# A hybrid encoder layer on one core: low halves of four row sums formed in gate and up, and the finishing of the last down chunk in a paced list

## The chip, the cores and the metric

The kernel runs on one core of a Trainium2 chip. The time is device microseconds of one execution, as the median of three runs. Five engines work beside each other, each in the order of its own queue: TensorE (PE; PEld is its weight load), VectorE (DVE), ScalarE (ACT), GpSimd (POOL) and SyncE (SP), which only issues transfers. ScalarE and GpSimd issue some transfers too.

## What is computed

```python
def hybrid_layer(x, conv_prev, S0, sc_prev, ...):
    h = rmsnorm(x, norm_mix_pre)
    P = h @ w_in
    ...
    mix = jnp.concatenate([o, sc_out.astype(x.dtype)], axis=-1) @ w_o
    x = x + rmsnorm(mix, norm_mix_post)

    h = rmsnorm(x, norm_ffn_pre)
    f = (jax.nn.silu(h @ w_gate) * (h @ w_up)) @ w_down
    x = x + rmsnorm(f, norm_ffn_post)
    return x, conv_new, S_new, sc_new
```

There are 2048 + 128 rows of 1024 columns, in 17 tiles of 128 rows; D_FF is 2816, in 22 blocks of 128. The change touches only the last line of the layer and the product by `w_down` before it.

## The kernel before

A float32 product is made of three products of a shorter type, fp32r: each operand is split into a high half (a cast by ScalarE) and a low half (the operand less its high half, a subtraction by GpSimd or VectorE), and high by high, high by low and low by high are added up in PSUM. Over that, products of 2 by 2 blocks are done with seven multiplications instead of eight (Winograd's form of Strassen's method), with sums of blocks as operands.

**Gate and up.** `gate_up` (L1417) runs over three groups of row tiles (`FGROUPS`: 6, 6 and 5 tiles, called group 0, 1 and 2) and in each over the 22 blocks f. A step has seven products of 12 matmuls (L1396), 384 columns wide in groups 0 and 1 and 320 in group 2. ScalarE copies three of the four PSUM banks out (L1428 to L1430) before TensorE adds to them again. The weights (`fw`) lie in a ring of 12 pairs of halves (`NWB`), seven for a step; in groups 1 and 2 four of seven are loaded ready from `fsplit` (L1369) and three are split on the spot (L1371, L1372). Every second step VectorE forms in the tile `pt` (one buffer) six of the seven row sums that the down projection needs as operands; they are stored to `partd` (L1433, on ScalarE's queue) in the next step. Between groups `ffn_prep` (L1319, L1320) splits the next group's inputs.

**Down.** The loop at L1699 takes the 22 blocks in five chunks; the last has six of them, so that a product has 3 x 3 = 9 matmuls, each 512 columns wide (L1574). In a chunk it goes over eight pairs of row blocks (three each of groups 0 and 1, two of group 2; the first two, the duo, alternate) and over a single block, which in the last chunk comes before the last pair. `down_pair` (L1616) loads the seven row sums (`ar`, L1564, three buffers), `split` (L1551) makes the halves `as` (ring of six, `NDA`): the cast on ScalarE (L1554), the low half in the last chunk on VectorE for product 0 and on GpSimd for products 1 to 6 (L1557). VectorE adds each product to the accumulators (L1534).

**Finishing.** In the last chunk a pair ends with `finish` (L1577) for each of its two row blocks. For each half of 512 columns: ScalarE's sum of squares (L1587), an addition of EPS in the first half (L1589), the product by the norm's gain (L1590). Then the two sums are added (L1593), GpSimd takes the power -1/2 (L1594), VectorE scales each half and adds the residual row `xr` (L1599), and the half is stored to `out_y` (L1601). `xr` is loaded from `x2d` (L1548, tag `dr`, four buffers). The final pair has its own order of steps: products 0, 1, 2, 3, 5, 4, 6, and parts of `finish` between them (L1644, L1650, L1651).

The order in the queues isn't written out in full: a scheduler with a model of the engines places the instructions, within the dependences and the `issue_after` marks.

```python
steps = ((b1, True, a4), (b2, True, a4), (b3, True, a4), (b4, True, a4), (b1, False, a1), (b2, False, a2), (b3, False, a3))
...
e = V if i in ((0,) if end else (0, 3)) or (duo and not ch and len(ready) < 2) else G
```

## Time and profile before

| | us |
|---|---|
| median of 3 runs (2452.22 to 2453.81) | 2452.97 |
| the profiled execution, its own time | 2450.11 |
| its span | 2448.2 |
| TensorE busy | 2424.2 (99%) |
| VectorE busy | 1620.6 (66%) |
| ScalarE busy | 1043.0 (43%) |
| GpSimd busy | 572.7 (23%) |

The span runs from the first to the last recorded instruction of the profiled execution; what the execution's own time has over it, 1.9 us, lies around it. TensorE's granted clock is 0.999 of full speed over the whole span. In a row of instructions, `fbank<-dw,as` means that `fbank` is written from `dw` and `as`; after `x` comes how many there are. The last down chunk takes the stretch from about 2307 us on, the last group of gate and up ends near 1960.

### The profile page before, as it was taken

What the parts mean: (1) busy time and instruction counts of PE and PEld (TensorE: products, weight loads), DVE (VectorE), ACT (ScalarE), POOL (GpSimd) and SP (SyncE); (2) the same over time, 40 slices, a digit from 0 to 9 for tenths busy, and PEclk for the clock granted to TensorE, in tenths of its full rate; (3) what the DMA queues carried; (4) which work ended last, traced back from release to release, by engine and by line L of the source; (5) the groups of instructions that cost most, each with busy time, mean ns of one, the idle gap of its engine ahead of it and who ended that gap; (6) DMA issues with size and microseconds to landing.
All of it is one profiled execution on the core that took longest, in us unless ns stands there. A gap on an engine that the chain in (4) does not pass through costs nothing.

```text
span 2448.2 us, 39317 instructions
## 1 busy us (share of the span) xinstructions
PE 2424.2 (99%) x14360; PEld 2219.0 (91%) x14360; DVE 1620.6 (66%) x3070; ACT 1043.0 (43%) x2335; POOL 572.7 (23%) x664
## 2 busy tenths in 40 slices
PE   9999999999999999999999999999999999999997
PEld 7888889999989988899999999999999988887876
DVE  7875755746667356888888744456555565677698
ACT  6645546546444333444343422224333355333343
POOL 1101001001110000156655200000000056456664
PEclk9999999999999999999999999999999999999999
DMA  7774655766776657698877888888998744333475
GB/s 271 260 252 167 218 194 198 247 220 231 271 252 247 214 177 230 200 341 297 291 257 256 293 258 263 257 251 271 312 294 278 248 142 122 117 107 120 140 232 175
DMA packets 263465, 561.38 MB, mean 229 GB/s; under 512 B 25188, under 2 KB 144680, under 8 KB 245992
## 3 DMA queue, kind: packets, MB, share of 16 engines
q1 hardware_dynamic: 147024, 487.24, 59.1%
q10 hardware_dynamic: 116024, 70.58, 9.6%
q8 instruction: 113, 1.85, 0.3%
q0 software_dynamic: 224, 1.05, 0.1%
q14 instruction: 80, 0.66, 0.1%
HBM read 400.09 MB, written 158.70 MB: 228 GB/s over the span
## 4 chain that ended last, share of the span: by engine, by line
PE 87%; DVE 6%; issue 2%; DMA 2%; POOL 2%; ACT 1%; DVEq 0%; ACTq 0%; POOLq 0%; SPq 0%
PE fbank L1396 35%; PE dbank L317 26%; PE fbank L1574 11%; PE dbank L1161 4%; PE tbank L1161 4%; DVE xr L1599 1%; DVE acc L1534 1%; PE tbank L375 1%; POOL as L1557 1%; PE gbank L598 1%; PE gbank L605 1%; POOL dw L1246 1%; PE obank L777 1%; PE gbank L769 1%; PE ftbank L1190 1%
## 5 line engine op out<-in xcount | busy, mean ns | idle before, releaser
L1396 PE MATMUL fbank<-xh,fw 128*128 128x384 f32 (+1 forms) x3696 | 897.5, 326 | 0.7 <-ACT m L1428 0.6
L317 PE MATMUL dbank<-hi,w 128*128 128x384 f32 (+1 forms) x2240 | 655.5, 363 | 1.5 <-ACT w L296 0.8
L1396 PEld LDWEIGHTS fbank<-xh,fw 128*128 128x128 f32 x3696 | 650.8, 188 | 1.4 <-ACT m L1428 0.9
L1396 PE MATMUL fbank<-xl,fw 128*128 128x384 f32 (+1 forms) x1848 | 601.9, 326 | 0.0
L317 PEld LDWEIGHTS dbank<-hi,w 128*128 128x128 f32 x2240 | 412.5, 188 | 42.6 <-issue 3.6
L1574 PE MATMUL fbank<-dw,as 128*128 128x512 f32 x1782 | 420.8, 392 | 5.4 <-DVE acc L1534 2.9
L1574 PEld LDWEIGHTS fbank<-dw,as 128*128 128x128 f32 x1782 | 333.0, 188 | 85.1 <-POOL as L1557 3.5
L317 PE MATMUL dbank<-lo,w 128*128 128x384 f32 (+1 forms) x1120 | 399.6, 357 | 0.3 <-DVE lo L232 0.3
L1396 PEld LDWEIGHTS fbank<-xl,fw 128*128 128x128 f32 x1848 | 346.9, 188 | 0.0
L317 PEld LDWEIGHTS dbank<-lo,w 128*128 128x128 f32 x1120 | 210.7, 188 | 16.7 <-DVE lo L232 0.6
L1557 POOL TENSOR_TENSOR as<-ar,as 128x256 fp32r<-128x256 f32 (+1 forms) x202 | 183.5, 919 | 177.7 <-ACT as L1554 162.0
L1534 DVE TENSOR_TENSOR acc<-acc,fbank 128x512 f32<-128x512 f32 x246 | 164.0, 681 | 90.6 <-PE fbank L1574 77.2
L1246 POOL TENSOR_TENSOR dw<-dr,dw 128x512 fp32r<-128x512 f32 x48 | 70.1, 1472 | 504.2 <-ACT dw L1244 503.9
L1554 ACT CAST as<-ar 128x256 fp32r<-128x256 f32 (+1 forms) x287 | 116.5, 427 | 165.7 <-PE fbank L1574 123.0
L1371 ACT CAST fw<-rg 128x512 fp32r<-128x512 f32 x124 | 77.2, 622 | 233.8 <-PE fbank L1396 136.3
L321 DVE SCALAR_TENSOR_TENSOR acc<-R,vec,acc 128x512 f32<-128x512 f32 (+2 forms) x180 | 121.0, 673 | 28.6 <-ACT acc L358 22.7
L1444 DVE TENSOR_TENSOR c<-u,fbank 128x384 f32<-128x384 f32 (+1 forms) x66 | 34.9, 528 | 97.8 <-PE fbank L1396 97.8
L1440 DVE TENSOR_TENSOR m<-m,m 128x384 f32<-128x384 f32 (+1 forms) x44 | 23.1, 526 | 84.3 <-ACT m L1430 84.1
L1447 ACT ACTIVATE c<-c 128x384 f32<-128x384 f32 (+1 forms) x66 | 33.4, 506 | 97.5 <-DVE c L1446 97.5
L1372 POOL TENSOR_TENSOR fw<-rg,fw 128x512 fp32r<-128x512 f32 x44 | 64.1, 1458 | 45.4 <-ACT fw L1371 45.1
L350 POOL COPY hist<-R 128x3 f32<-128x3 f32 x60 | 20.0, 334 | 218.6 <-ACT R L326 169.3
L1442 ACT ACTIVATE m<-fbank 128x384 f32<-128x384 f32 (+1 forms) x66 | 31.2, 473 | 91.3 <-PE fbank L1396 74.4
(398 smaller groups left out, 3567.1 us busy)
## 6 DMA issues: line engine op xcount, KB each, us to landing
w<-wsplit SPq DMA_DIRECT2D x105, 1024.0 KB, 5.1
fw<-fsplit SPq DMA_DIRECT2D x188, 512.0 KB, 4.9
fsplit<-fw SPq DMA_DIRECT2D x94, 512.0 KB, 3.6
partd<-pt ACTq DMA_DIRECT2D x86, 384.0 KB, 5.8
rg<-in_w_gu SPq DMA_DIRECT2D x62, 512.0 KB, 4.3
wsplit<-w SPq DMA_DIRECT2D x28, 1024.0 KB, 5.2
wr<-in_w_in SPq DMA_DIRECT2D x34, 512.0 KB, 6.2
ar<-partd SPq DMA_DIRECT2D x43, 384.0 KB, 3.2
```

The lines of the kernel that those rows point to most:

```text
L317: T.matmul(ps[:, :c], l[:, k, :], r[k][:, :c], start=(k == 0 and r is hi and l is wh), stop=(k == KD - 1 and l is wl))
L321: r = V.scalar_tensor_tensor(acc, raw(d), w[:, d:d + 1], acc, op0=ALU.mult, op1=ALU.add)
L1161: T.matmul(pss[n], m_[:, j, :], w_[k][:, n * 512:(n + 1) * 512], start=(k == 0 and ci == 0), stop=(k == KD - 1 and ci == 2))
L1246: e.tensor_tensor(out=w[1], in0=v, in1=w[0].bitcast(F32), op=ALU.subtract)
L1371: A.copy(w[:, 0], v)
L1372: e.tensor_tensor(out=w[:, 1], in0=v, in1=w[:, 0].bitcast(F32), op=ALU.subtract)
L1396: T.matmul(ps, w_[:, c], b_[k][:, :hw], start=(first and k == 0 and ci == 0), stop=(k == KH - 1 and ci == 2), skip_group_check=not first)
L1444: V.tensor_add(c21, u2, b3)
L1534: return eng.tensor_tensor(out=dst, in0=dst, in1=ps, op=ALU.add)
L1554: ins = A.copy(a[:, 0, :n], v)
L1557: e.tensor_tensor(out=a[:, 1, :n], in0=v, in1=a[:, 0, :n].bitcast(F32), op=ALU.subtract)
L1574: T.matmul(ps, a[:, x_, q * P:(q + 1) * P], w[y_], start=(start and q == 0 and ci == 0), stop=(q == c - 1 and ci == 2), skip_group_check=True)
```

## The change

- In gate and up, for the last chunk of groups 1 and 2, the low halves of row sums 1 to 4 (`NLOW`) are formed one step after the sums: ScalarE casts each into a spare buffer of `a11` or `a21`, GpSimd subtracts it in place in `pt`, and a step later the result is stored to a new array `lowd` on ScalarE's queue. That is three bundles in group 1 and two in group 2, of whose third part nothing is formed ahead (`low_end`). In the down chunk `split` loads these low halves by SP into `as`; group 1 needs no subtraction for products 1 to 4 any more, group 2 one of 128 columns.
- The finishing steps become single functions. Those on VectorE go into a list, `todo`; after each addition to an accumulator `pace` issues up to two of them, and stops behind a factor. The sums of squares stay with the step that ends their half. EPS is added in the instruction that adds the two sums.
- In the last pair `issue_after` marks fix the order of products 5, 4 and 6 on TensorE and of the steps on VectorE; the gained halves go into the accumulators of the first pair instead of the tile `xm`, and only the first half of the last row block is stored by ScalarE's queue.

```diff
 NDA = 6
+NLOW = 4
...
+    lowd = {gi: dram.tile([len(g) // 2, P, NLOW, len(FCHUNKS[-1]) // 2, P], F32, name=f"lowd{gi}")
+            for gi, g in enumerate(FGROUPS) if gi}
...
+        def low_end(gi):
+            return len(FCHUNKS[-1]) // 2 - (gi + 1 == len(FGROUPS))
...
+                while lstores:
+                    nc.scalar.dma_start(**lstores.pop(0))
...
+            if lows:
+                pgi, pq, pp = lows.pop()
+                pw = len(FGROUPS[pgi]) * P // 2
+                his = [fb.tile([P, HW], F32R, tag=nm, name="hi_" + nm, bufs=2) for nm in ("a11", "a21")]
+                with tc.issue_after(gmark["A"].ins), tc.issue_after(gmark["V"].ins):
+                    for i in range(NLOW):
+                        A.copy(his[i % 2][:, :pw], pp[:, i, :pw])
+                        G.tensor_tensor(out=pp[:, i, :pw], in0=pp[:, i, :pw], in1=his[i % 2][:, :pw].bitcast(F32), op=ALU.subtract)
+                for j in range(len(FGROUPS[pgi]) // 2):
+                    lstores.append(dict(out=lowd[pgi][j, :, :, pq, :], in_=pp[:, 0:NLOW, j * P:(j + 1) * P]))
...
+                if gi and ch + 1 == len(FCHUNKS) and q < low_end(gi):
+                    lows.append((gi, q, pt))
...
-        def split(v, e, first=False):
+        def split(v, e, first=False, low=None):
             n = v.shape[-1]
             a = da.tile([P, 2, MC * P // 2], F32R, tag="as", name="as", bufs=NDA)
+            m = 0
+            if low is not None:
+                gi, j, i = low
+                m = low_end(gi) * P
+                nc.sync.dma_start(out=a[:, 1, :m].bitcast(F32), in_=lowd[gi][j, :, i].rearrange("p q c -> p (q c)")[:, :m])
             ins = A.copy(a[:, 0, :n], v)
             if first:
                 cast[:] = [ins]
-            e.tensor_tensor(out=a[:, 1, :n], in0=v, in1=a[:, 0, :n].bitcast(F32), op=ALU.subtract)
+            if m < n:
+                e.tensor_tensor(out=a[:, 1, m:n], in0=v[:, m:], in1=a[:, 0, m:n].bitcast(F32), op=ALU.subtract)
...
+                    ins = T.matmul(ps, a[:, x_, q * P:(q + 1) * P], w[y_], start=(start and q == 0 and ci == 0),
+                                   stop=(q == c - 1 and ci == 2), skip_group_check=True)
+            return ins
-        def finish(v, places, first=0, apart=False):
...
+        todo, mark_f = [], {}
+
+        def pace(ins):
+            for _ in range(2):
+                if todo:
+                    with tc.issue_after(ins.ins):
+                        if todo.pop(0)():
+                            break
+
+        def behind(f, *a):
+            with tc.issue_after(mark_f["V"].ins):
+                f(*a)
+
+        def finish(v, places, first=0, m=None, front=nc.sync):
+            m = m or v
+            row = []
+            ss = dn.tile([P, 2], F32, tag="ss2", name="fss2", bufs=6)
+            r = dn.tile([P, 1], F32, tag="fr", name="fr", bufs=6)
+
+            def load():
+                row.append(dr.tile([P, D], F32, tag="dr", name="xr", bufs=4))
+                for p0, (r0, n) in places:
+                    load_x2(row[0], p0, r0, n)
+
+            def square(h):
                 A.activation(junk, v[h], AF.Square, scale=D ** -0.5, accum_out=ss[:, h:h + 1])
+
+            def gain(h):
+                mark_f["V"] = V.tensor_mul(m[h], v[h], gpo[:, 512 * h:512 * h + 512])
 
             def factor():
+                mark_f["V"] = V.scalar_tensor_tensor(ss[:, 0:1], ss[:, 0:1], EPS, ss[:, 1:2], op0=ALU.add, op1=ALU.add)
                 G.tensor_tensor(out=r, in0=ss[:, 0:1], in1=neghalf[:, 0:1], op=ALU.pow)
+                return True
+
+            def scale(h):
+                c, xt = slice(512 * h, 512 * h + 512), row[0]
+                mark_f["V"] = V.scalar_tensor_tensor(xt[:, c], m[h], r, xt[:, c], op0=ALU.mult, op1=ALU.add)
+                for p0, (r0, n) in places:
+                    (front if h == first else nc.sync).dma_start(out=yr[r0:r0 + n, c], in_=xt[p0:p0 + n, c])
+
+            def end():
+                return [factor, lambda: scale(first), lambda: scale(1 - first)]
+
+            return load, square, gain, factor, scale, end
...
+            if end:
+                r1, r2 = rows(u)
+                done = acc[pairs[0]] if final else None
+                load2, square2, gain2, factor2, scale2, end2 = finish((a2, a4), [(0, r2)], 1, final and (done[:, 0], done[:, 1]))
+                load1, square1, gain1, factor1, scale1, end1 = finish((a1, a3), [(0, r1)], 0, final and (done[:, 2], done[:, 3]),
+                                                                      nc.scalar if final else nc.sync)
...
+                low = (gi, j, i - 1) if end and gi and 1 <= i <= NLOW else None
+                a = ready[i] if i < len(ready) else split(parts[i], e, duo and not ch, low)
+                with tc.issue_after(pe.ins) if final and i > 3 and i != 5 else ExitStack():
+                    pe = product(b, ch, a, i, mid)
...
+                elif i < 4:
+                    ins = acc_add(a4, b)
+                    if i < 3 or not final:
+                        pace(ins)
+                    else:
+                        while todo:
+                            todo.pop(0)()
+                    if i == 3:
+                        V.tensor_sub(a2, a4, a2)
+                        mark_f["V"] = V.tensor_sub(a3, a4, a3)
+                        square2(1)
+                        if final:
+                            behind(gain2, 1)
+                        else:
+                            todo.append(lambda: gain2(1))
+                elif final:
+                    with tc.issue_after(mark_f["V"].ins):
+                        mark_f["V"] = acc_add(a1, b) if i == 4 else V.tensor_sub(dst, dst, b)
+                    if i == 5:
+                        square2(0)
+                        behind(gain2, 0)
+                        behind(factor2)
+                    elif i == 4:
+                        square1(0)
+                        behind(scale2, 1)
+                        behind(gain1, 0)
+                    else:
+                        square1(1)
+                        behind(gain1, 1)
+                        behind(factor1)
+                        behind(scale2, 0)
+                        behind(scale1, 0)
+                        behind(scale1, 1)
+                elif i == 4:
+                    ins = acc_add(a1, b)
+                    square1(0)
+                    todo.append(lambda: gain1(0))
+                    pace(ins)
+                elif i == 5:
+                    ins = V.tensor_sub(a2, a2, b)
+                    square2(0)
+                    todo.extend([lambda: gain2(0), *end2()])
+                    pace(ins)
                 else:
+                    ins = V.tensor_sub(a3, a3, b)
+                    square1(1)
+                    todo.extend([lambda: gain1(1), *end1()])
+                    pace(ins)
...
-            if end and not last:
-                V.tensor_sub(a2, a4, a2)
-                V.tensor_sub(a3, a4, a3)
-                r1, r2 = rows(u)
-                finish_all((a1, a3), [(0, r1)])
-                finish_all((a2, a4), [(0, r2)])
```

VectorE at the end of the second pair of group 1 (`acc_1`, the first rows of `acc_2` are the next pair's), before:

```order
L1671 TENSOR_TENSOR acc_1_21173<-acc_1_21173 128x512
L1534 TENSOR_TENSOR acc_2_21260<-acc_2_21260,fbank 128x512
L1590 TENSOR_TENSOR acc_1_21173<-acc_1_21173,gpo 128x512
L1593 TENSOR_TENSOR fss_24405<-fss_24405 128x1
L1589 TENSOR_SCALAR fss_24420<-fss_24420 128x1
...
L1599 SCALAR_TENSOR_TENSOR xr<-acc_1_21173,fr,xr 128x512 x2
L1593 TENSOR_TENSOR fss_24420<-fss_24420 128x1
L1557 TENSOR_TENSOR as<-ar,as 128x384
L1534 TENSOR_TENSOR acc_2_21260<-acc_2_21260,fbank 128x512
L1599 SCALAR_TENSOR_TENSOR xr<-acc_1_21173,fr,xr 128x512 x2
```

and now:

```order
L1736 TENSOR_TENSOR acc_1_21238<-acc_1_21238,fbank 128x512
L1632 TENSOR_TENSOR acc_1_21238<-acc_1_21238,gpo 128x512
L1635 SCALAR_TENSOR_TENSOR fss_24360<-fss_24360 128x1
L1741 TENSOR_TENSOR acc_1_21238<-acc_1_21238,fbank 128x512
L1641 SCALAR_TENSOR_TENSOR xr<-acc_1_21238,fr,xr 128x512 x2
L1554 TENSOR_TENSOR acc_2_21325<-acc_2_21325,fbank 128x512
L1632 TENSOR_TENSOR acc_1_21238<-acc_1_21238,gpo 128x512
L1635 SCALAR_TENSOR_TENSOR fss_24362<-fss_24362 128x1
L1554 TENSOR_TENSOR acc_2_21325<-acc_2_21325,fbank 128x512
L1641 SCALAR_TENSOR_TENSOR xr<-acc_1_21238,fr,xr 128x512 x2
L1583 TENSOR_TENSOR as<-ar,as 128x384
```

Behind the first addition to `acc_2` (L1534 before, L1554 now) there stood three gains (L1590) and four scalings of the pair that ended; now there stand one gain (L1632) and two scalings (L1641), and between two additions at most two finishing steps on 512 columns. The split `as` (L1557, now L1583), for product 0 of the pair after `acc_2`'s, keeps its place between `acc_2`'s second and third addition.

TensorE in the last pair (the weights `sA` and `sB` belong to product 5, `sC` and `sD` to product 6), before:

```order
L1574 MATMUL fbank<-dw,as 128x512 x60
L1574 MATMUL fbank<-sA,as 128x512
L1574 MATMUL fbank<-sB,as 128x512
L1574 MATMUL fbank<-sA,as 128x512
L1574 MATMUL fbank<-dw,as 128x512 x6
L1574 MATMUL fbank<-sC,as 128x512
```

and now:

```order
L1600 MATMUL fbank<-dw,as 128x512 x54
L1600 MATMUL fbank<-sA,as 128x512
L1600 MATMUL fbank<-sB,as 128x512
L1600 MATMUL fbank<-sA,as 128x512
L1600 MATMUL fbank<-dw,as 128x512 x12
L1600 MATMUL fbank<-sC,as 128x512
```

Six matmuls of product 4, which stood ahead of those of product 5, now stand behind them.

SP in group 1 of the last chunk, now (`lowd` loads are new; the other kinds are there before too):

```order
L1578 DMA as<-lowd_133 128x384
L1590 DMA ar<-partd_4_122 128x768
L1643 DMA out_y<-xr 128x512 x2
L1578 DMA as<-lowd_133 128x384
L1568 DMA xr<-x2d_167 128x1024
L1578 DMA as<-lowd_133 128x384
L1590 DMA ar<-partd_4_122 128x768
L1578 DMA as<-lowd_133 128x384
L1568 DMA xr<-x2d_164 128x1024
L1643 DMA out_y<-xr 128x512 x2
L1590 DMA ar<-partd_4_122 128x1152
```

The loads of low halves stand between the stores of results and the loads of row sums and residual rows.

## Rows read from the trace of the kernel before

**Rows 1.** The page, part 1: busy time, share of the span, instructions.

```profile
PE 2424.2 (99%) x14360; PEld 2219.0 (91%) x14360; DVE 1620.6 (66%) x3070; ACT 1043.0 (43%) x2335; POOL 572.7 (23%) x664
```

**Rows 2.** Stretches: length; PE, PEld, DVE, ACT, POOL busy (instructions); clock, DMA share, GB/s.

```profile
2340.00:2355.00 15.00, 15.00 (x67) 12.32 (x66) 15.00 (x27) 6.28 (x16) 9.45 (x10) 1.00 0.65 215
2355.00:2370.00 15.00, 15.00 (x68) 12.29 (x67) 15.00 (x24) 5.66 (x15) 7.39 (x8) 1.00 0.79 260
2370.00:2385.00 15.00, 13.60 (x57) 10.06 (x56) 14.66 (x23) 4.43 (x12) 9.13 (x8) 1.00 0.79 258
```

**Rows 3.** Waits of TensorE's weight loads from 2305 on: total us, times, longest.

```profile
PEld fbank L1574 <- DVE acc L1534: 2.5, 4, 1.5
PEld fbank L1574 <- DVE as L1557: 1.4, 2, 0.8
PEld fbank L1574 <- issue: 1.2, 1, 1.2
PEld fbank L1574 <- ACT as L1554: 0.9, 2, 0.5
PEld fbank L1574 <- DVE accs L1534: 0.5, 1, 0.5
```

**Rows 4.** Order of time, weight loads without a stall: start, length of all.

```profile
2364.98 8.82 PEld L1574 LDWEIGHTS fbank<-dw,as 128*128 128x128 f32 x39
```

**Rows 5.** Order of time, the end: start, length, engine, line [idle before, releaser].

```profile
2435.39 1.52 PE L1574 MATMUL fbank<-dw,as 128*128 128x512 f32 x6
...
2436.64 0.68 DVE L1644 TENSOR_TENSOR acc<-acc,fbank 128x512 f32<-128x512 f32 x1
...
2439.91 1.41 DVE L1599 SCALAR_TENSOR_TENSOR xr<-xm,fr,xr 128x512 f32<-128x512 f32 x2 [0.67 <-POOL fr L1594]
...
2441.24 0.68 DVE L1644 TENSOR_TENSOR acc<-acc,fbank 128x512 f32<-128x512 f32 x1
...
2443.66 1.42 DVE L1599 SCALAR_TENSOR_TENSOR xr<-xm,fr,xr 128x512 f32<-128x512 f32 x2 [0.73 <-POOL fr L1594]
```

**Rows 6.** VectorE and GpSimd by line: ns min/median/max, or busy us and mean ns.

```profile
L1534 DVE TENSOR_TENSOR acc<-acc,fbank x59: 671/675/689, 2304.3 to 2437.2; 128x512 f32<-128x512 f32 x59
...
L1599 DVE SCALAR_TENSOR_TENSOR xr<-acc,fr,xr x28: 734/822/1514, 2342.1 to 2426.7; 128x512 f32<-128x512 f32 x28
...
L1599 DVE SCALAR_TENSOR_TENSOR xr<-acc,fr,xr 128x512 f32<-128x512 f32 x28 | 29.1, 1076 | 0.1
...
L1557 POOL TENSOR_TENSOR as<-ar,as 128x384 fp32r<-128x384 f32 x48 | 57.9, 1223 | 26.9 <-ACT as L1554 13.4 <-issue 12.8 <-POOL fr L1594 0.5
...
L1557 POOL TENSOR_TENSOR as<-ar,as 128x256 fp32r<-128x256 f32 x154 | 125.6, 825 | 150.8 <-ACT as L1554 148.6 <-PE fbank L1574 1.8
```

**Rows 7.** The page, part 6: transfers, KB each, us from issue to landing.

```profile
ar<-partd SPq DMA_DIRECT2D x43, 384.0 KB, 3.2
```

**Rows 8.** Stretches of gate and up, groups 1 and 2, columns as in rows 2.

```profile
1655.00:1670.00 15.00, 15.00 (x88) 15.00 (x87) 7.55 (x14) 4.19 (x8) 0.00 (x0) 1.00 0.80 246
1685.00:1700.00 15.00, 15.00 (x88) 15.00 (x87) 12.96 (x31) 11.71 (x29) 0.00 (x0) 1.00 0.92 313
1725.00:1737.00 12.00, 12.00 (x84) 12.00 (x84) 6.47 (x13) 3.85 (x8) 0.00 (x0) 1.00 0.99 323
```

**Rows 9.** Order of time, ScalarE's queue in group 1: three stores of `pt`.

```profile
1620.28 1.89 ACTq L1433 DMA_DIRECT2D partd<-pt  x3
```

**Rows 10.** Waits of SP, and landing of weights, 1600 to 1960 us.

```profile
SPq L1369 <- PE fbank L1396: 186.9, 105, 4.9
...
fw<-fsplit SPq DMA_DIRECT2D x115, 512.0 KB, 5.0
```

**Rows 11.** Order of time, the change from group 1 to group 2.

```profile
1703.49 0.89 DVE L1320 TENSOR_TENSOR xl<-fh,xh 128x320 fp32r<-128x320 f32 x2
...
1703.02 0.43 ACT L1428 COPY m<-fbank 128x320 f32<-128x320 f32 x1 [1.25 <-PE fbank L1396]
```

**Rows 12.** Waits of SP from 2296 on: total us, times, longest.

```profile
SPq L1601 <- DVE xr L1599: 38.8, 20, 5.6
```

87 lines of the change are left out of this document (28 added, 59 removed).

## The prediction, made before the change had run

> **What bounds the kernel now.** I read the page first. TensorE is busy for 2424.2 of 2448.2 us [rows 1], so what a change of order can win lies in the 24 us that are left; the change touches the last 140 us. Second, the stretches of the last down chunk: from 2340 to 2370 VectorE is busy 15.00 us in 15, then 14.66, and in that third stretch TensorE first falls short, with 57 matmuls where the two before had 67 and 68 [rows 2]. Third, the waits of TensorE's weight loads, which show a stall better than the modelled ends of matmuls: 2.5 + 1.4 + 1.2 + 0.9 + 0.5 = 6.5 us from 2305 on, nearly all behind VectorE, or behind a cast that ScalarE got to late [rows 3]. Without stalls a load follows the one before by (8.82 - 0.19) / 38 = 0.227 us [rows 4], so a product of nine matmuls takes 2.04 us and a pair of row blocks (seven products) 14.3 us.
>
> Fourth, the end, in order of time. The last matmuls begin at 2435.39 and end 1.52 us later, at 2436.91. VectorE is then still at the subtraction for product 5 (2436.64), waits for the two sums of squares, scales two halves at 2439.91, and only at 2441.24 subtracts the last product [rows 5]. So 4.33 us pass between TensorE's end and the step that needs it, and 6.96 us from there to the end of the span at 2448.2, which are a chain: square, factor, scale, store.
>
> **Why VectorE is full.** Its additions that read PSUM take 0.671 to 0.689 us, always. Its scaling `xr`, with two operands in SBUF, takes 0.734 at best, 1.514 at worst and 1.076 in the mean of the 28 of the chunk's pairs, which is 28 x (1.076 - 0.734) = 9.6 us more than it need be; GpSimd spends 48 x 1.223 = 58.7 us on `as` in the same time [rows 6]. The Trainium skill gives a reason ("SBUF — State Buffer", section "SBUF: two separate sides"): a VectorE instruction with two SBUF inputs and a GpSimd instruction that reads SBUF lock each other out for a whole instruction. The two rows agree with it: the form that reads PSUM doesn't stretch, the other does.
>
> **The change, part by part.**
>
> *Low halves ahead of time, in the down chunk.* For the three pairs of group 1, four GpSimd subtractions each disappear; for the two of group 2 they shrink from 384 to 128 columns. 384 columns cost 1.223 us and 256 cost 0.825 [rows 6], a step of 0.398, so 128 are estimated at 0.43. GpSimd loses 12 x 1.223 + 8 x 0.79 = 21.0 of its 58.7 us. In proportion, the scaling gets back 9.6 x 21.0 / 58.7 = 3.4 us of VectorE time. By the lock alone up to 21.0 us of VectorE's waiting could go. It makes no difference to the sum, since TensorE waits 6.5 us in all.
>
> In their place SP issues 20 loads. A load of twice the size lands in 3.2 us [rows 7]. The ring `as` holds six, so a slot comes free five products, 10.2 us, before its product starts: 7.0 us to spare. Cost 0; if SP is held up for longer than that, the excess is TensorE's (second rival).
>
> *Low halves ahead of time, in gate and up.* Added are five bundles of four casts on ScalarE, four subtractions on GpSimd and two or three stores on ScalarE's queue. TensorE there is busy in every microsecond [rows 8], so nothing can be won and something lost. ScalarE: four casts (0.43 us for 320 columns [rows 11], so some 0.52 for 384) and three issues in 1.89 us [rows 9] come to 4.0 us a bundle, beside 4.19 busy in 15 [rows 8]: covered. Its copies out of PSUM come between the casts, and TensorE needs each three products (over 5 us) after it could start. VectorE: it writes `pt` next only once the bundle's stores have landed, so some wait is new; behind it stand the next weights' subtractions, and the weight ring is 12 deep with 7 in use a step. DMA: a bundle of group 1 is 4 x 128 x 384 x 4 B = 0.79 MB, at the 323 GB/s of the fullest stretch, 0.99 busy [rows 8], 2.4 us of all queues. Weights are loaded when a slot comes free, 11 products before use: 11 x 12.0 / 7 = 18.8 us in group 2 (84 matmuls, seven products, in 12.0 us), against 5.0 us to land, and SP waits on TensorE for slots, 105 times, 186.9 us [rows 8, 10]: the loads are paced by TensorE, not by the DMA engines. Cover 13 us, price 2.4.
>
> The one tight place is the change of groups at 1685 to 1700: VectorE 12.96 us in 15, 2.04 idle [rows 8]. There a bundle of 4 x 1.223 = 4.9 us of GpSimd would, if VectorE stood still for all of it, make the new group's inputs 2.9 us late. They are done at 1703.49 + 0.89 = 1704.4. ScalarE's copy at 1703.02 follows the new group's first product, so its sixth, which uses the last but one of them, starts near 1703.0 + 4 x 1.71 = 1709.9 [rows 11]. 2.9 us fit into 5.5. By the skill's lock that lateness is to be expected; by the rows it costs nothing. Gate and up: 0, bounds 0 and 2.9.
>
> *Paced finishing.* No work goes but the 17 additions of EPS to one column. What moves: behind the next pair's first addition VectorE had three gains and four scalings of the old pair to do, 3 x 0.675 (a gain taken as long as an addition) + 4 x 1.076 = 6.3 us with the additions behind them; now one gain and two scalings. How late it was, the waits tell: TensorE waited for VectorE's `as`, which stands in VectorE's order right behind addition 1, while product 0 of the next pair, which uses it, comes five products after product 1; and for additions, which TensorE needs only four products on, when it adds to the same bank again [rows 3]. So VectorE was four products behind, as far as the banks let it. Now a slot's worst load is an addition and two scalings, 0.675 + 2 x 0.734 = 2.1 us against 2.04, and slots with less follow, so it should stay within one product. Of the 6.5 us I let 5.0 go; the rest is left to the duo's casts and GpSimd, which keeps all six subtractions there. Bounds: 2.5 (only what stands behind additions goes) to 6.5.
>
> *Last pair in a fixed order.* TensorE now does product 5 whole, then 4, then 6; before, six matmuls of 4 stood ahead of it. With E for TensorE's end, the additions of product 3 can start at E - 6.1. Four VectorE steps (add, two subtractions, gain) at 0.675 end at E - 3.4; subtraction 5 and gain end at E - 2.05; addition 4, scaling, gain (0.675 + 0.75 + 0.675) end at E + 0.1. The last subtraction starts about 0.1 to 0.3 us after E, not 4.33. The chain behind it keeps its length: the one scaling of the other half put into it (0.73) runs while GpSimd works out the factor. Gain 4.0, bounds 2.0 (VectorE still waits for a factor once) and 4.3.
>
> **Sum.** -5.0 - 4.0 + 0 = -9.0 us. The profiled execution took 2450.11, and would take 2441.1. The median of the three runs is 2.86 above it, so the forecast is 2452.97 - 9.0 = **2444.0 us**. About 0.2% (4.9 us) is what a measurement of this kernel can tell from no change.
>
> **Rivals.**
>
> *VectorE stays the bound.* For it: 15.00 in 15 for 30 us, and the first three pairs (group 0) keep all GpSimd work, while their finishing now starts earlier, beside it. Against it: stalls begin only at 2370, when the backlog of that stage has run up, and there GpSimd's load falls most. Then only the lower bounds come true, -2.5 - 2.0 = -4.5: 2448.5.
>
> *SP becomes the bound: slower.* SP works in order. Stores of `y` wait there for VectorE's scaling, 20 times, up to 5.6 us [rows 12], and the loads of low halves now stand behind them: SP's order puts loads between stores of the previous pair. A scaling late by more than 7.0 us makes a low half late, TensorE waits, and the additions and scalings behind it come later still. Two such waits in a row (11.2 us) cost 11.2 - 7.0 = 4.2 us in each of five pairs, 21 us, and the gain in stalls doesn't come: -4.0 + 21 = +17: 2470. It decides from 7.0 us on; one wait of 5.6 fits, and in the new order scalings stand one or two products behind their factor, so I don't expect it.
>
> *Gate and up pay.* Each of five bundles holds up the weights, or VectorE, for its whole price: 3 x 2.4 + 2 x 1.6 = 10.4 us, less 9.0: 2454.4, no change. Against it: 13 us of cover.
>
> *The lock at the change of groups* is not covered: +2.9, so 2446.9.
>
> **How the numbers follow.** Forecast 0.66 (its own range 2441.7 to 2447.0: all stalls and 4.3 gone, 10.8 less and half a microsecond for the runs' spread, or the mean of the lower bounds and the forecast); VectorE still the bound 0.14 (2446.5 to 2450.5); the lock 0.05; gate and up 0.07; SP 0.08. The range 2441.7 to 2450.5 takes in the first three. Faster by over 0.2%, below 2448.1: 0.66 + 0.05 + 0.4 x 0.14 = 0.76 less a little for bounds that add up badly, 0.74. Within 0.2%: 0.17. Slower: 0.09.
>
> **What would show it.** In the profile after: weight loads from 2305 on wait less than 2 us; scaling `xr` well under 1.076 us in the mean; the last subtraction within 0.5 us of the last matmul's end, and some 7.0 us from there to the end; gate and up as long as before, TensorE without idle time, though VectorE waits for stores before `pt`. It is wrong if TensorE's loads wait for DMA `as`, if the `as` loads leave SP late, if idle time shows before L1396, or if VectorE is still full from 2370 on.

## The result and the profile after

The changed kernel takes 2457.36 us (median of 22 executions, 2450.94 to 2466.27) against 2452.15 for the kernel before (22 executions, 2448.83 to 2454.19). The ratio is 1.0021, 95% interval 1.0015 to 1.0027: **slower by 5.2 us**, just over what a measurement of this kernel can tell from no change. The forecast was 2444.0. The profiled execution of the changed kernel took 2453.93 us, with a span of 2452.0; that of before, 2450.11 and 2448.2. One execution of e1 below and one of the kernel before beside it took over 2648 us, at a lower granted clock, and are left out of the ratios.

Three places tell the story, and a fourth goes nearly as forecast. First gate and up, in the first steps of group 2, where the last bundle of group 1 is stored, in order of time (start, length, engine, line; in brackets the idle time before and what ended it):

```profile
1727.00 1.99 ACTq L1441 DMA_DIRECT2D lowd<-pt  x3
...
1735.33 0.49 DVE L1467 TENSOR_TENSOR pt<-c,m 128x320 f32<-128x320 f32 x1 [4.56 <-DMA lowd<-pt]
...
1736.71 0.43 ACT L1435 COPY m<-fbank 128x320 f32<-128x320 f32 x1 [5.47 <-DVE pt L1468]
...
1737.19 0.19 PEld L1399 LDWEIGHTS fbank<-xh,fw 128*128 128x128 f32 x1 [2.04 <-ACT m L1435]
```

This is a chain over four queues. ScalarE issues the stores of the low halves from 1727.00 on. VectorE stands 4.56 us before the product that it writes into `pt`, until they have landed. Its next product into `pt` (L1468) is the last reader of the one buffer `m7`, and ScalarE may not copy a PSUM bank into that buffer before; TensorE may not add to the bank before the copy. So TensorE idles for 2.04 us in a stage where it had not idled at all. The DMA engines are at a share of 1.01 and 343 GB/s in the 5 us before (first row; the last row is the kernel before):

```profile
1730.00:1735.00 5.00, 5.00 (x36) 5.00 (x36) 0.69 (x1) 1.24 (x4) 0.00 (x0) 1.00 1.01 343
1735.00:1740.00 5.00, 3.22 (x22) 2.96 (x22) 4.57 (x10) 0.75 (x2) 0.00 (x0) 1.00 0.72 221
...
1735.00:1740.00 5.00, 5.00 (x36) 5.00 (x35) 2.56 (x5) 1.16 (x4) 0.00 (x0) 1.00 1.07 385
```

(Stretches, columns as in [rows 2].) In the same 5 us from 1735 on the kernel before had 36 matmuls, here there are 22. VectorE stands before `pt` for such a landing at three of the five bundles, TensorE behind it at two.

The second place is the change from gate and up to down (gate and up end near 1972 in the kernel before), again in order of time:

```profile
1969.48 1.42 ACTq L1441 DMA_DIRECT2D lowd<-pt  x2
...
1976.64 0.49 DVE L1486 TENSOR_TENSOR pt<-a,a 128x320 f32<-128x320 f32 x1 [5.82 <-DMA lowd<-pt]
...
1983.97 2.07 PE L1600 MATMUL fbank<-dw,as 128*128 128x512 f32 x4 [3.40 <-DVE as L1583]
...
1986.27 0.63 PE L1600 MATMUL fbank<-sB,as 128*128 128x512 f32 x1
...
1986.70 0.63 PE L1600 MATMUL fbank<-sA,as 128*128 128x512 f32 x1
...
1987.13 0.63 PE L1600 MATMUL fbank<-sC,as 128*128 128x512 f32 x1
```

VectorE waits 5.82 us for the stores of the last bundle before it may write `pt` for the last row sums of group 2. Behind it in its order stand the first low halves of down, and TensorE waits 3.40 us for those. Then a second loss follows: matmuls start 0.43 us apart instead of 0.227 [rows 4], since the granted clock has dropped to 0.57 of full speed in the mean of the 5 us from 1985 on, that is, for most of it at 1.2 GHz instead of 2.4:

```profile
1980.00:1985.00 5.00, 1.60 (x6) 0.97 (x5) 4.93 (x6) 3.90 (x9) 4.83 (x5) 0.75 0.50 160
1985.00:1990.00 5.00, 5.00 (x15) 3.90 (x14) 5.00 (x8) 1.33 (x4) 1.74 (x3) 0.57 0.51 185
1990.00:1995.00 5.00, 5.00 (x24) 4.14 (x23) 4.48 (x8) 2.98 (x7) 3.61 (x4) 1.00 0.64 210
```

The kernel before idled there too, 1.39 us in front of the weight load at 1978.27, and kept a clock of 1.00:

```profile
1978.27 0.77 PEld L1574 LDWEIGHTS fbank<-dw,as 128*128 128x128 f32 x4 [1.39 <-DVE as L1557]
...
1980.02 0.39 PE L1574 MATMUL fbank<-sC,as 128*128 128x512 f32 x1
```

By the first matmul that reads `sC` the changed kernel is 7.1 us behind (1980.0 before, 1987.1 after). Just ahead of the last chunk, near 2303, it is 7.7 behind, counted by matmuls with the same number from the start.

The third place is the last down chunk. These are the waits of the weight loads from 2305 on, beside [rows 3], and in order of time what lies behind the longest:

```profile
PEld fbank L1600 <- DMA as<-lowd: 3.3, 2, 2.8
PEld fbank L1600 <- ACT as L1579: 0.3, 1, 0.3
```

```profile
2357.01 0.42 SPq L1643 DMA_DIRECT2D out_y<-xr  x1
2357.49 0.42 SPq L1578 DMA_DIRECT2D as<-lowd  x1
...
2358.48 2.69 SPq L1578 DMA_DIRECT2D as<-lowd  x1
...
2364.14 3.86 PEld L1600 LDWEIGHTS fbank<-dw,as 128*128 128x128 f32 x11 [2.79 <-DMA as<-lowd]
```

```profile
2364.00:2367.00 3.00, 2.86 (x8) 2.29 (x9) 2.75 (x5) 1.12 (x3) 1.64 (x3) 0.63 0.98 360
```

The ten stalls of before are gone. In their place the first pair of group 1 waits for its loaded low halves: SP issues the first behind stores of finished rows, and one issue alone takes 2.69 us. All twenty loads landed in 3.6 to 8.6 us, 5.1 in the median. The granted clock falls here as well (0.63 from 2364 to 2367). The matmul that starts at 2361.39, in front of the wait, is 7.65 us behind the one with its number in the kernel before (2353.74), and that at 2370.22 is 11.95 behind (2358.27): the wait and the low clock cost 4.3 us. The stalls of before that are gone, nearly all behind this place, give 4.7 back, and the last matmul is 7.3 us behind. So next to nothing of the 6.5 us is left as a gain.

The end did nearly what it should, beside [rows 5]:

```profile
2437.18 1.42 DVE L1641 SCALAR_TENSOR_TENSOR xr<-accs,fr,xr 128x512 f32<-128x512 f32 x2
...
2438.52 0.68 DVE L1554 TENSOR_TENSOR acc<-acc,fbank 128x512 f32<-128x512 f32 x1
...
2442.66 1.52 PE L1600 MATMUL fbank<-dw,as 128*128 128x512 f32 x6
...
2444.67 0.68 DVE L1714 TENSOR_TENSOR acc<-acc,fbank 128x512 f32<-128x512 f32 x1
...
2446.44 0.99 POOL L1636 TENSOR_TENSOR fr<-fss,neghalf 128x1 f32<-128x1 f32 x1 [3.08 <-DVE fss L1635]
...
2447.47 1.42 DVE L1641 SCALAR_TENSOR_TENSOR xr<-acc,fr,xr 128x512 f32<-128x512 f32 x2 [0.44 <-POOL fr L1636]
```

TensorE ends at 2444.18, the last subtraction starts 0.49 us later (4.33 before), and the span ends 7.8 us after TensorE, 11.3 before. So the profiled executions add up: 7.3 late, less 3.5 in the tail, is the 3.8 us between the spans.

### The profile page after: what moved, and what is told of

Read it like the earlier page. It is cut to its first block, busy times and chain, and to the rows that moved or that the text cites. A ratio compares the mean times of both kernels' runs of the same rounds, so it can differ in the third digit from the quotient of the medians.

```text
span 2452.0 us, 39398 instructions
## 1 busy us (share of the span) xinstructions
PE 2427.8 (99%) x14360; PEld 2222.4 (91%) x14360; DVE 1618.6 (66%) x3053; ACT 1050.3 (43%) x2355; POOL 567.5 (23%) x672
## 5 line engine op out<-in xcount | busy, mean ns | idle before, releaser
L1554 DVE TENSOR_TENSOR acc<-acc,fbank 128x512 f32<-128x512 f32 x232 | 155.0, 682 | 89.1 <-PE fbank L1600 75.7
L1583 POOL TENSOR_TENSOR as<-ar,as 128x256 fp32r<-128x256 f32 (+2 forms) x190 | 161.6, 860 | 181.6 <-ACT as L1579 178.7
L1479 POOL TENSOR_TENSOR pt<-pt,hi_a 128x384 f32<-128x384 f32 (+1 forms) x20 | 20.2, 1045 | 403.0 <-DMA fw<-fsplit 282.1
```

What stands on the lines that cost most here:

```text
L1554: return eng.tensor_tensor(out=dst, in0=dst, in1=ps, op=ALU.add)
L1583: e.tensor_tensor(out=a[:, 1, m:n], in0=v[:, m:], in1=a[:, 0, m:n].bitcast(F32), op=ALU.subtract)
```

## The experiments

Theory at the outset: the changed kernel loses its time to `pt`, which is held until the stores of the low halves land. Rivals: the added work of ScalarE and GpSimd in gate and up; late loads in down; a paced list that gains nothing. Twelve kernels were timed, each beside the kernel before on the same chip:

| run | low halves | finishing of the earlier pairs | last pair | us | before | ratio, 95% interval |
|---|---|---|---|---|---|---|
| e1 | none | paced | new | 2451.90 | 2451.73 | 1.0001 [0.9992, 1.0010] |
| e2 | formed in `pt`, stored, not loaded | old | old | 2462.19 | 2451.73 | 1.0042 [1.0030, 1.0054] |
| e3 | other values loaded, none formed | paced | new | 2446.21 | 2451.73 | 0.9977 [0.9968, 0.9986] |
| e4 | own buffer, loaded | paced | new | 2446.58 | 2451.73 | 0.9976 [0.9967, 0.9986] |
| e5 | as e4, loads on ScalarE's queue | paced | new | 2447.15 | 2451.59 | 0.9980 [0.9971, 0.9988] |
| e6 | as e4 | old | old | 2445.19 | 2451.59 | 0.9971 [0.9960, 0.9982] |
| e7 | formed in `pt`, not stored | old | old | 2453.28 | 2451.59 | 1.0003 [0.9994, 1.0012] |
| e8 | as e4, but not in the first pair of group 1 | paced | new | 2446.92 | 2451.59 | 0.9980 [0.9972, 0.9989] |
| e9 | as e4 | list emptied at once | new | 2447.74 | 2452.18 | 0.9984 [0.9976, 0.9993] |
| e10 | none | list emptied at once | new | 2453.60 | 2452.18 | 1.0007 [0.9998, 1.0016] |
| e11 | as e4 | old | new | 2442.49 | 2452.83 | 0.9957 [0.9944, 0.9969] |
| e12 | none | old | new | 2449.83 | 2452.83 | 0.9988 [0.9979, 0.9997] |

Where a buffer of their own holds the low halves (e4, e5, e6, e8, e9, e11), the weight ring has 11 pairs; in the others it has 12.

**e1, the finishing alone.** From the changed kernel:

```diff
-                if gi and ch + 1 == len(FCHUNKS) and q < low_end(gi):
-                    lows.append((gi, q, pt))
...
-                low = (gi, j, i - 1) if end and gi and 1 <= i <= NLOW else None
+                low = None
```

> The paced list and the fixed order alone: no low halves are formed ahead, none are loaded. Theory A (the paced part gains what was forecast, the low halves give it back): of the 6.5 us of stalls in the last down chunk some 2 remain because GpSimd keeps all its subtractions, and the stretch from the last matmul to the end is 7.5 to 8 us where it was 11.3; so 7 to 8 us faster than before, 2445. Rival B (VectorE stays the bound while GpSimd keeps its work, so pacing without the low halves is worth little): stalls as before, only the end gains, 3 to 4 us faster, 2449.

2451.90: nothing, slower than either theory had it. The tail is 8.0 us, but TensorE now waits more in the chunk than the 6.5 us of before:

```profile
PEld fbank L1598 <- issue: 8.2, 8, 1.8
PEld fbank L1598 <- DVE acc L1552: 1.7, 1, 1.7
PEld fbank L1598 <- ACT as L1577: 0.2, 1, 0.2
```

VectorE's scaling got slower, not faster (by line: busy us, mean ns of one; 32 here, since the last pair's four, at 0.75 us, now count with the others; [rows 6] has 1076 for 28):

```profile
L1639 DVE SCALAR_TENSOR_TENSOR xr<-acc,fr,xr 128x512 f32<-128x512 f32 x32 | 36.0, 1160 | 1.0 <-POOL fr L1634 0.4
```

So the new finishing, by itself, gives back in stalls what the last pair's order gains.

**e2, the low halves alone.** The kernel before with the changed kernel's `gate_up`: bundles are formed and stored; down is as before and reads none of them.

> The low halves are formed and stored in gate and up as in the change, but the down chunk is that of before and doesn't load them. Theory A (the store of the low halves holds the only buffer of the row sums, VectorE waits for it in order, and ScalarE's copies and the first splits of the down projection wait behind VectorE): 2.0 us once in group 2, 2.4 us more at the change to the down projection, and some 2 us for matmuls at the lower granted clock after it: 5 to 7 us slower than before, 2457 to 2459, with VectorE waiting for the landing of the stores 4 to 6 us at those two places. Rival B (gate and up are covered, the loss lies in the loads of the down chunk): within 1 us of before, 2452.

2462.19, 10.4 us slower, where theory A had 5 to 7. Waits of the weight loads, 1600 to 2000 us:

```profile
PEld fbank L1594 <- DVE as L1577: 3.8, 1, 3.8
PEld fbank L1399 <- ACT m L1435: 3.1, 1, 3.1
PEld fbank L1594 <- ACT as L1574: 0.8, 1, 0.8
PEld fbank L1399 <- ACT m L1436: 0.5, 1, 0.5
```

They are the two places of the changed kernel, 8.2 us against 1.4 in the kernel before, and the granted clock falls behind both (0.93 from 1725 to 1750, 0.83 from 1990 to 2000).

**e3, loads without forming.** As e1, but the low halves of the last chunk are loaded from places in `partd` that hold other values; so the low parts of those products are not the kernel's.

```diff
-                nc.sync.dma_start(..., in_=lowd[gi][j, :, i]...)
+                nc.sync.dma_start(..., in_=partd[gi][-1][j, :, i + 1]...)
```

> The paced list, and in the down chunk the 20 loads and the missing subtractions as in the change; but nothing is formed in gate and up: the loads fetch row sums of the same size instead of their low halves, so the output is not that of the reference in those products' low parts. Theory A (loads that come late cost 3 to 4 us once, with the lower clock behind it, but gate and up costs nothing here): 4 to 6 us faster than before, 2446 to 2448, with one wait of TensorE for a loaded low half of 2 to 3 us near the first pair of group 1. Rival B (the loads are the whole loss of the change): as slow as the change, 2456 to 2458.

2446.21, 5.5 us below before, and 5.7 below e1, which finishes in the same way: with GpSimd freed the down chunk does gain. TensorE waits for loads four times there, 5.2 us, where one wait was expected. Gate and up is as before (1775 matmuls from 1700 to 1960; 1774 before, 1758 in the changed kernel).

**e4, a buffer of their own.** The low halves are written to a new tile for three sums and a spare buffer for the fourth, so that `pt` is free once GpSimd has read it. To make room the weight ring goes from 12 to 11.

```diff
-NWB = 12
+NWB = 11
...
+                plow = fb.tile([P, NLOW - 1, HW], F32, tag="plow", name="plow")
+                outs = [plow[:, i, :pw] for i in range(NLOW - 1)] + [his[1][:, :pw].bitcast(F32)]
...
-                        G.tensor_tensor(out=pp[:, i, :pw], ...)
+                        G.tensor_tensor(out=outs[i], ...)
```

> The whole change, but the low halves are written to a buffer of their own (three sums) and to the spare buffer of a column block (the fourth), so that the buffer of the row sums is free as soon as GpSimd has read it; to make room the ring of weights has 11 pairs instead of 12. As many bytes are stored and loaded as in the change. Theory A (the buffer's wait): VectorE no longer waits for these stores, TensorE has no idle time in group 2, and the time is that of the loads-only kernel, 4 to 6 us faster than before, 2446 to 2448. Rival B (the traffic itself, or ScalarE's and GpSimd's extra work, holds up gate and up): TensorE still waits in group 2 or at the change to down, 2455 to 2458.

2446.58: the whole loss is gone, 10.4 us from one edit (+5.2 to -5.2 beside before), and the kernel beats both. VectorE waits nowhere for `lowd`. Left in the last chunk:

```profile
PEld fbank L1605 <- DMA as<-lowd: 2.6, 2, 2.3
PEld fbank L1605 <- ACT as L1584: 0.3, 1, 0.3
```

**e7, formed but not stored.** As e2 without the stores; nothing else differs.

```diff
-                for j in range(len(FGROUPS[pgi]) // 2):
-                    lstores.append(dict(out=lowd[pgi][j, :, :, pq, :], in_=pp[:, 0:NLOW, j * P:(j + 1) * P]))
```

> The low halves are formed in gate and up as in the changed kernel, in the buffer of the products, but never stored, and the last chunk loads none and finishes as before: the same output as before, with 16 casts of ScalarE and 16 subtractions of GpSimd more. The same with the stores was 10.4 us slower than before (e2, 2462.2 us). Theory A (the buffer is held until the stores have landed, 5 to 7.5 us after their issue): without them VectorE's waits for the buffer in gate and up shrink to what GpSimd's four subtractions take, and the time is that of before to 3 us over it, 2451 to 2455 us. Theory B (the added work of ScalarE and GpSimd holds VectorE or the product's copies up): 2457 us or more, with TensorE's waits of 1700 to 2000 us as in e2, some 8 us.

2453.28, ratio 1.0003, theory A. The five bundles of casts and subtractions are still there, and TensorE's waits are back to the kernel before's, 1600 to 2000 us:

```profile
PEld fbank L1592 <- DVE as L1575: 1.4, 1, 1.4
PEld fbank L1399 <- ACT m L1436: 0.2, 1, 0.2
```

So the stores cost about 9 of e2's 10.4 us. The added work has 1.7 left at the median, which can't be told from zero (the interval is -1.5 to +2.9 us). e7 takes the stores away and their traffic with them; e4 keeps as many bytes and frees `pt`. Both lose the waits, so it is the hold of `pt` that costs and not the traffic.

**e5, loads on another queue, and e8, none in the first pair.** Both from e4:

```diff
-                nc.sync.dma_start(out=a[:, 1, :m].bitcast(F32), in_=lowd...)
+                nc.scalar.dma_start(out=a[:, 1, :m].bitcast(F32), in_=lowd...)
```

> Beside the kernel with a buffer of its own for the low halves (e4), one thing moves: the loads of the low halves in the last down chunk are issued from ScalarE's queue instead of SP's. In the changed kernel they stand on SP behind the stores of finished rows and the loads of the residual, and the first pair's are issued some 6 us after their slot was free. Theory A (SP's order makes them late): TensorE's waits for these loads, 2.6 us in e4, fall under 1 us; the time is 1.5 to 3 us below e4, about 2444 us. Theory B (the landing itself is slow, while the DMA engines are over 0.9 busy): the waits stay at 2 to 3 us and the time at e4's, 2445.5 to 2448 us. Theory C (an issue on ScalarE delays the casts behind it, which TensorE needs sooner): waits for ScalarE's casts take their place, and the time is e4's or up to 3 us over it.

```diff
-                low = (gi, j, i - 1) if end and gi and 1 <= i <= NLOW else None
+                low = (gi, j, i - 1) if end and gi and u != (1, 0) and 1 <= i <= NLOW else None
```

> Beside e4: the first pair of the first of the two groups loads no low halves; GpSimd forms them there as in the kernel before. In the changed kernel and in e4 all of TensorE's waits for these loads lie at that pair, where SP still issues the stores of group 0 and the loads of its residual. Theory A (only that pair's loads come too late): the wait of 2.6 us goes, ScalarE's and GpSimd's small waits stay under 1 us, and the time is 1 to 3 us below e4, about 2444.5 us. Theory B (GpSimd's subtractions of that pair stretch VectorE's row sums as in the kernel before): waits for VectorE's subtractions of 1 to 3 us take its place, and the time stays at e4's, 2446 to 2448 us.

2447.15 and 2446.92, both as e4 within their intervals. In e5 the wait for loads shrinks to 1.6 us, and 1.4 us for ScalarE's casts and 1.1 of "issue" come in its place; in e8 it shrinks to 0.7, and 4.7 us of "issue" come. Neither first theory held; e5 fits its third, with waits for ScalarE's casts in the place of those for loads. The loads of e5 leave 5.6 us earlier (from 2344.2 on, 2349.8 in e4) and the time stays: the late loads are where the chunk's trouble shows, not all that causes it.

**e6, the low halves with the old finishing.** The kernel before with e4's `gate_up`, `split` and loads, and its ring of 11.

> The low halves of e4 (own buffer, loaded in the last chunk), with the finishing work of the kernel before: no paced list, the old order of the last pair. With the kernel before (2451.7 us), the pacing alone (2451.9 us) and both (2446.6 us) this fills a square of two by two. Theory A (the two only pay together: pacing takes 3.3 us off the tail and gives them back in stalls unless GpSimd is freed): the loads alone remove a part of the 6.5 us of stalls, 2 to 4 us of the time, so 2447.5 to 2450 us. Theory B (the loads do it all): 2446 to 2447 us, with the tail as before, some 11 us from TensorE's end to the end of the span. Theory C (nothing without the pacing, since VectorE stays the one that is late): 2451 to 2452.5 us.

2445.19: no slower than e4, without any of the new finishing; the second theory, a little below its range. The tail is 10.1 us. TensorE hardly waits (from 2305 on):

```profile
PEld fbank L1605 <- ACT as L1584: 0.2, 1, 0.2
PEld fbank L1605 <- DMA as<-lowd: 0.2, 1, 0.2
```

```profile
L1630 DVE SCALAR_TENSOR_TENSOR xr<-acc,fr,xr 128x512 f32<-128x512 f32 x28 | 20.8, 784 | 0.3
```

The scaling's mean falls from 1076 to 784 ns, 8.2 us of VectorE over 28, so the low halves take the stalls away alone. The first loads are issued at 2344.56 here, 2349.82 in e4, and land no sooner (6.0 us in the median, 5.8 in e4).

**e9 and e10, the list emptied at once,** with the low halves (from e4) and without (from e1):

```diff
-            for _ in range(2):
-                if todo:
-                    with tc.issue_after(ins.ins):
-                        if todo.pop(0)():
-                            break
+            while todo:
+                todo.pop(0)()
```

> Beside e4 (own buffer, loads of low halves, all of the new finishing) the list is not paced: at each step it is emptied at once. The fixed order of the last pair stays. With the old finishing (e6) TensorE waited 0.4 us after 2305 us and the span ended 10.1 us after TensorE; with the paced list and the fixed order (e4) it waited 2.9 us and the span ended 8.0 us after it; both took 2445.2 to 2446.6 us. Theory A (the pacing brings the waits, since SP's loads stand behind stores that it puts off; the order of the last pair brings the tail): waits under 1 us and a tail of 8.0 us, so 2442.5 to 2444.5 us, the best so far. Theory B (the pacing is what shortens the tail, or it is the fixed order that makes the loads late): 2445 to 2447 us.

> No low half is formed or loaded (GpSimd subtracts as before), the list is emptied at once at each step, and the last pair has its fixed order: the last pair's order alone beside the kernel before. The pacing and the order together (e1) gained 3.3 us in the tail and lost as much in the last chunk (10.1 us of waits against 6.5). Theory A (the pacing alone is what costs): waits of TensorE of 5 to 7.5 us as before, the tail 8.0 us, so 2448 to 2449.5 us. Theory B (the waits come from the other changes of the finishing, such as the earlier loads of the residual): 10 us of waits again and 2451 to 2453 us.

2447.74 and 2453.60, in both 0.6 to 0.7 us above the range of the second theory and far from the first: pacing isn't what costs. Without it the waits grow to 6.1 us in e9 (2.9 in e4) and are still 10.6 us in e10 (10.1 in e1); e10's are these:

```profile
PEld fbank L1598 <- ACT as L1577: 5.2, 4, 1.8
PEld fbank L1598 <- issue: 3.7, 3, 2.1
PEld fbank L1598 <- DVE acc L1552: 1.7, 2, 1.3
```

**e11 and e12, the last pair's order alone,** with the low halves and without. All other pairs finish as before, behind the pair's own additions (their sums and factors have six buffers instead of two):

```diff
+                if final and i > 3:
+                    with tc.issue_after(mark_f["V"].ins):
+                        mark_f["V"] = acc_add(a1, b) if i == 4 else V.tensor_sub(dst, dst, b)
...
             if end and not last:
                 V.tensor_sub(a2, a4, a2)
                 V.tensor_sub(a3, a4, a3)
                 r1, r2 = rows(u)
                 finish_all((a1, a3), [(0, r1)])
                 finish_all((a2, a4), [(0, r2)])
```

> Beside e6 (low halves in a buffer of their own and loaded, finishing as before) only the last pair takes the new fixed order; all pairs before it keep the finishing of the kernel before, which stands behind the pair's own additions. Emptying the list at once instead of pacing it (e9) did not take TensorE's waits away: 6.1 us with loads, 10.6 us without (e10), against 0.4 us in e6. Theory A (the new finishing's place inside the pair, its subtractions and products ahead of the additions that free banks, brings the waits; the last pair's order alone brings the tail): waits under 1 us, a tail of 8.0 us instead of 10.1 us, so 2 us below e6, 2442.5 to 2444 us. Theory B (the order of the last pair holds TensorE up itself, so that the shorter tail is paid for ahead of its end): 2445 to 2447 us, with TensorE's end 1 to 3 us later than in e6.

> The last pair's new order alone beside the kernel before: no low half is formed or loaded, all other pairs finish as before. Theory A: waits of some 6.5 us as before, a tail of 8.0 us instead of 11.3, so 2447.5 to 2449.5 us. Theory B (the order holds TensorE up in the last pair): TensorE ends 1 to 3 us later than in before and the time is 2450 to 2453 us.

2442.49 is the first theory's. **e11 is 10.3 us faster than the kernel before** and the best of all. Its waits and its end:

```profile
PEld fbank L1605 <- DMA as<-lowd: 1.4, 2, 0.7
PEld fbank L1605 <- ACT as L1584: 0.3, 1, 0.3
```

```profile
2433.69 1.52 PE L1605 MATMUL fbank<-dw,as 128*128 128x512 f32 x6
...
2435.25 0.69 DVE L1725 TENSOR_TENSOR acc<-acc,fbank 128x512 f32<-128x512 f32 x1
```

With TensorE's end at 2435.21 and the span's at 2442.8 the tail is 7.6 us. TensorE ends 2.7 us later than in e6's trace, but it is 2.4 us behind the kernel before near 483 us already (e6: 0.4), long before the first low half is formed. In the last pair, from 2421 on in the kernel before, both gain the same 1.3 us on it; so the order doesn't hold TensorE up here.

e12's 2449.83 lies between its two theories. Its waits add up to 5.6 us, and one of them is in the last pair:

```profile
2431.69 0.94 PE L1603 MATMUL fbank<-dw,as 128*128 128x512 f32 x3 [2.37 <-DVE acc L1557]
...
2436.64 1.52 PE L1603 MATMUL fbank<-dw,as 128*128 128x512 f32 x6
```

TensorE ends at 2438.16, 1.25 us later than in the kernel before, and the tail is 9.4 us, not 8.0. At this place the kernel before waits 1.5 us, for an addition of VectorE too (the longest wait in [rows 3]), and e11, where the low halves are loaded, not at all.

## Why the prediction was wrong

The runs make a chain from the kernel before to the changed one, each link one part of the change. Medians, each less that of the kernel before timed beside it:

| link | from, to | us |
|---|---|---|
| low halves ready when down needs them | before, e6 | -6.4 |
| last pair's order | e6, e11 | -3.9 |
| new finishing in the earlier pairs | e11, e4 | +5.2 |
| low halves kept in `pt` until stored | e4, changed kernel | +10.4 |
| all (links rounded) | | +5.2 |

A link has an uncertainty of some 3 to 4 us, by the intervals of the two ratios that it stands between, so the two in the middle stand out from zero only just, or not quite. Beside them, the order of the last pair alone (e12) is -3.0, and the new finishing without low halves is +3.2 with pacing (e12 to e1) and +4.4 without (e12 to e10). The last link also takes the ring from 11 to 12, which wasn't run by itself.

In the prediction's own terms, the two profiled executions give 7.7 us for gate and up and the change to down, where it had 0; -0.4 for the stalls of the last chunk, where it had -5.0; and -3.5 for the tail, where it had -4.0: together +3.8 for -9.0. Two terms failed.

**Gate and up: the first step that failed.** The prediction put it at 0, bounds 0 and 2.9; it cost 10.4 by the medians and 7.7 in the profiled execution, one of the faster ones. It saw the wait ("it writes `pt` next only once the bundle's stores have landed, so some wait is new"), and named as what stands behind it "the next weights' subtractions, and the weight ring is 12 deep". That was the wrong follower. What stood behind it was the product L1468, which frees `m7` for ScalarE's copy out of PSUM, and, at the end of group 2, the first low halves of down: buffers with a depth of one in gate and up, and operands that TensorE needs at once in down. The slack of that copy, "three products (over 5 us)", was set only against ScalarE's casts; the copy stood 5.47 us behind L1468. The wait itself was never priced either: from the issue at 1727.00 to VectorE's start at 1735.33 the stores held `pt` for 8.3 us, while a step of group 2 has 12.0 us in all. The Trainium skill's fit for one transfer ("SBUF — State Buffer", section "The DMA setup-cost knee": about 2 us and the bytes at 436 GB/s) would give 2.6 us as an estimate for a store of 256 KB; the trace has 6.1 in the median of thirteen, with the DMA engines at a share of 0.66 to 0.97 while they landed, and the measurement decides. The rival "Gate and up pay" had this sign, but priced the DMA engines' share (2.4 us a bundle, five bundles) where the cost was the hold of one buffer, at two of five bundles; that its price came to 10.4 as well is chance. It stood at 0.07.

**Low halves in down: right, for more than was said.** The forecast gave 5.0 us of stalls to this and the paced finishing together. The low halves alone brought 6.4 (e6). The reason held: GpSimd relieved, VectorE's scaling falls to 784 ns. The Trainium skill's rule on the two engines' lock ("SBUF — State Buffer", section "SBUF: two separate sides") agrees in direction, and the measured size is 8.2 us of VectorE, between the proportion's 3.4 and the 21.0 of whole instructions.

**Loads: mis-sized.** The prediction took 3.2 us to land from another transfer [rows 7]; these took 5.1 to 6.0 in the median. With the old finishing (e6, e11) that hardly mattered. In the changed kernel TensorE waited 2.8 us once, 4.3 with the low clock behind it, where the prediction had 0. That is the second rival's mechanism at a small price, and in the medians it is part of the link "new finishing".

**Paced finishing: the second step that failed, with the wrong sign.** "Now a slot's worst load is an addition and two scalings ... so it should stay within one product" took the scaling at its best, 0.734 us. The new finishing of the earlier pairs costs 3 to 5 us, and the traces show the scalings stretched:

```profile
L1646 DVE SCALAR_TENSOR_TENSOR xr<-acc,fr,xr 128x512 f32<-128x512 f32 x32 | 29.1, 946 | 1.0 <-POOL fr L1641 0.4
```

That is e4, with the last pair's four; without them it is 975 ns in e4, 977 in the changed kernel and 1219 in e1, where the old finishing has 784 and 782 (e6, e11) and 1076 (before). Those of the 28 scalings during which GpSimd ran no subtraction into `as` took 740 to 745 ns in the mean in each of these runs. Those beside one took 964 to 1323, and they are 14 in e4, 23 in e1, 5 in e6 and 17 in the kernel before. So the new places of the scalings lie beside GpSimd's subtractions more often, as the first rival had it for the first three pairs ("their finishing now starts earlier, beside it"); it stood at 0.14. An addition and two scalings at 0.977 are 2.6 us, over the 2.04 of a product. e9 and e10 show that the list's pacing is not the cause. Which of the other things that moved is (the two subtractions, the gains and the residual's loads now stand inside the pair, ahead of its last additions), and whether the stretched scalings are all of the 3 to 5 us, was not separated and stays open.

**Last pair: right.** Forecast -4.0, bounds 2.0 and 4.3; measured 3.5 in the changed kernel's tail, -3.9 and -3.0 in the runs. The last subtraction started 0.49 us after TensorE, not 0.1 to 0.3: VectorE began the pair's last steps at 2438.52, 0.44 later than 6.1 us ahead of TensorE's end, behind the scalings of the single block. And the chain behind the subtraction did not keep its length, 7.33 us for 6.96, because GpSimd's power took 0.99 us beside the scaling put there, for 0.55.

One slip in the numbers changes nothing: the mean of the lower bounds and the forecast is 2446.2, with half a microsecond 2446.7, where the prediction's own range ends at 2447.0.

## What to carry to other kernels

When a tile is kept longer, price it by the tile's next writer and by what stands behind that writer on its engine, down to the first buffer with a depth of one; here a ring of 12 elsewhere covered nothing of it. Time a hold from the store's issue to its landing under the load of that stage, not from bytes over bandwidth. And split a change of several parts before you judge it: here parts that won 10 us and parts that lost over 15 sat in one diff.

## What the runs showed that was not expected

- An idle time of TensorE can cost more than its length. After 3.84 us without a weight load the granted clock was 0.50 of full speed from 1984 to 1989, matmuls stood 0.43 us apart instead of 0.227, and TensorE was 2.4 us further behind the kernel before when the clock was back. After 2.79 us the clock fell as well (0.63 from 2364 to 2367); after 2.04 and after 1.39 it stayed at 1.00. So a wait that looks like 3.8 us is one of over 6.
- One issue of a transfer on SP took 2.69 us where the twenty had 0.385 in the median, with the DMA engines full (1.01 busy, 366 GB/s from 2360 to 2364).
- The changed kernel's executions spread over 15.3 us, those of before over 5.4, and the nine of e4, which moves as many bytes without holding `pt`, over 4.1. Why the hold spreads them isn't shown, since one execution of each is profiled.
